# Stated orders of issue in the FFN and the recurrence of a hybrid HGRN2 and attention step

## The chip, the cores and the metric

The kernel runs on one core of a Trainium2 chip. The metric is device time in microseconds of one execution, the median of several; a separate profiled execution left the trace. The core's engines work side by side, each through its own instructions in a fixed order: TensorE (PE, with its weight loads PEld), VectorE (DVE), ScalarE (ACT), GpSimd (POOL) and SyncE (SP, which here issues transfers).

## What is computed

One layer of a diffusion backbone in float32 on 256 context ("prompt") and 1024 latent ("sample") tokens, width 1024: 1280 tokens in all. Cut to the parts that matter here:

```python
h = rms_norm(x, norm_mix_w) * (1 + sc1) + sh1          # sc, sh, g from adaln(c, w_ada)
z = h @ w_in                                            # hq, hf_fwd, hf_bwd, hi, hg, q, k, v, gl
o_a = block_attention(q, k_all, v_all)                  # latent: 512 cached + 1024 latent + context keys
# HGRN2, both directions, 4 heads of 128, chunks of 32:
f = lb + (1 - lb) * sigmoid(h_f);  k = 1 - f;  a = cumsum(log f) in the chunk
scores = tril((q e^a) (k e^-a)^T);   o = scores v + (q e^a) S;   S' = e^a_last S + (k e^(a_last - a))^T v
o_h = rms_norm(o_fwd + o_bwd) * silu(hg)
g = sigmoid(gl);  merged = g0 * (o_h @ w_ho) + g1 * (o_a @ w_ao)
x = x + g1 * (merged @ w_out)
x = x + g2 * (square(relu(norm2(x) @ w_ff1)) @ w_ff2)
y = rms_norm(x, final_norm_w)
```

Outputs are y for both kinds of token, the context's keys and values, and the final context states of the recurrence (`new_state_hgrn`, 2 directions x 4 heads).

## The kernel before

Every float32 operand of a large product is split into a high part (`hi`, on ACT) and a rest (`lo`, on DVE; both in `split`, L277 and L278), and each product is three matmuls: hi·hi, hi·lo, lo·hi (L306 to L308, L323 to L325). A weight block is loaded by `wraw` (1 MB, two buffers), split in halves by `w_oc` into `wsp` tiles (six buffers), and then used.

PE runs in the order in which the program is written. On DVE, ACT and POOL a scheduler sets the order when the kernel is built, from dependencies and priorities: `tc.high_priority(offset)` pulls the instructions inside it ahead. SP's order of transfers also comes from there, until the Strassen part, from where on it is written out. At run time each engine takes its instructions strictly in the order so set.

The stages, in us of the profiled execution's span:

- **Front**, 0 to 150: adaLN, first norm, projections for attention.
- **Attention**, 150 to 718: units of one head and 256 queries in 200 steps of 256 keys in all, each step with scores, maximum, exponential, transposition of the probabilities (`ps_t`, L735), their split (`pTh` on ACT, `pTl` on DVE L739) and the products with the values (L750, L751). At a unit's end the sum `oa` (L760) goes out. The work is a list of events in order of their step; between events `fill.to(...)` lets a *filler* put as many other matmuls on PE as its share of the total (277 estimated us) says. The filler `fz` here is the projections for the recurrence: `z_tok`, whose results pass through tiles `ze` (L849).
- **Recurrence**, 718 to 1003 (`hgrn`): 24 units `HUnit`, per head (direction, token tile) = (0,0), (0,1), (1,1), (1,0), (0,2), (1,2); tiles 0 and 1 are the latent tokens, 512 each, tile 2 the 256 context tokens. `prep` of unit i+1 is issued ahead of unit i's matmuls: it loads f (`uf`) and q (`uq`), runs two scans on DVE (`ucp`, the decay from the chunk's start, and `usf`, to its end), computes small tables of chunk products `um` and `udec`, k = 1 − f on POOL (L883), k·`usf` on POOL (L911), and that times two rows of `um`: one on POOL (in `uf`'s tile, for the scores), one on DVE (L907, in `usf`'s tile). The latter, called the *keyed product* in what follows, is transposed on PE by `keys_t` (L936) and copied by ACT to `ukt`. Two of three query products `uw` run on POOL, one on DVE. Then come the matmuls `scores` (masked to `usm`), `states_` (running states `ust`) and `out` (`uo`). The filler `fg` between them is the projection of the gates (`z_ch`).
- **Rest of the gates, merge, output projection**, 1003 to 1270.
- **FFN1, prompt pass**, 1270 to 1372: 16 turns i, each with two halves of 24 matmuls of a weight block just split; results squared and combined in `at` (DVE, L1378 to L1380). Beside it DVE and ACT form and split the sums of activations that the next stage needs: `sums1`, twelve parts, a part for every turn i = 3 to 14.
- **FFN1, Strassen part** for the latent tokens, 1372 to 1680: blocks of products over sums of blocks, X, Y and Z being banks of results; `u2` = Y + s1 (L1451) must be there before Y is used again (L1437).
- **FFN2**, 1680 to 2052, with chains P1 to P7 that end in residual additions, and the final norm (`square`, `final`) under and behind the last of them.

Of the kernel before, what the change touches and what calls it, by code (L numbers as in the profile page):

```python
# [15 lines left out]
P = 128  # L16
# [28 lines left out]
def build(ctx, tc, I, O, C):  # L45
# [230 lines left out]
    def split(hi, lo, raw):  # L276
        s_.activation(hi, raw, AF.Copy)  # L277
        v.tensor_tensor(lo, raw, f32(hi), op=ALU.subtract)  # L278
# [8 lines left out]

    def w_oc(raw, half, kcs=KC):

        hi, lo = wsp((P, kcs, P)), wsp((P, kcs, P))  # L290
        split(hi, lo, raw[:, :, half * P:(half + 1) * P])
        return hi, lo
# [37 lines left out]
    def z_ch(c0, consume):  # L330

        raw = wraw(I["w_in"], KC, c0)
        for half in range(2):
            wt = w_oc(raw, half)
# [323 lines left out]
    class Unit:  # L658
# [83 lines left out]
        def value(self, p2):  # L742
# [17 lines left out]
            v.tensor_tensor(oa, pv[d0:d0 + 64, 0:256], tm[d0:d0 + 64, 0:256], op=ALU.add)  # L760
# [4 lines left out]
    NORM = [g_, v]  # L765
    q_at, o_at = {}, {}
# [20 lines left out]
    def attention(fill):  # L787
# [68 lines left out]
    class HUnit:  # L856


        def __init__(self, h, d, t):
            self.h, self.d, self.t = h, d, t  # L860
            self.n, self.nb = TT[t][1], NB[t]

            self.zero = None if t < 2 else 0 if d == 0 else self.nb - 1

        def prep(self):
# [6 lines left out]
            c, e = S(name="ucp"), S(name="usf")  # L872
            if d == 0:
# [8 lines left out]
            k = self.k = f  # L882
            g_.tensor_scalar(k[:, 0:n], f[:, 0:n], -1.0, 1.0, op0=ALU.mult, op1=ALU.add)  # L883

# [7 lines left out]
            v.tensor_copy(out=Mf[:, 0:nb, 1:12:5], in_=Dv[:, :, 0:3])  # L892
            v.tensor_tensor(Mf[:, 0:nb, 2:8:5], Dv[:, :, 0:2], Dv[:, :, 1:3], op=ALU.mult)
            v.tensor_tensor(M[:, 0:nb, 0, 3], M[:, 0:nb, 0, 2], Dv[:, :, 2], op=ALU.mult)

            v.tensor_copy(out=M[:, 0:nb, 3, 2], in_=Dv[:, :, 3])
            for cc in (1, 0):
                v.tensor_tensor(M[:, 0:nb, 3, cc], M[:, 0:nb, 3, cc + 1], Dv[:, :, cc + 1], op=ALU.mult)
            v.reciprocal(M[:, 0:nb, 4, :], Dv)
            self.dec = T(4, "udec")  # L900
            v.tensor_tensor(self.dec[:, 0:nb], M[:, 0:nb, 3, 0], Dv[:, :, 0], op=ALU.mult)

            def mul4(out, in0, w, eng):
# [3 lines left out]
                eng.tensor_tensor(out[:, 0:n].rearrange("p (b c i) -> p b c i", c=4, i=32),  # L907
                                  in0[:, 0:n].rearrange("p (b c i) -> p b c i", c=4, i=32),
                                  mm.unsqueeze(3).broadcast_to([P, nb, 4, 32]), op=ALU.mult)

            g_.tensor_tensor(e[:, 0:n], k[:, 0:n], e[:, 0:n], op=ALU.mult)  # L911
            mul4(k, e, 4, g_)
            mul4(e, e, 3, v)
            self.ke = e
# [18 lines left out]
        def keys_t(self):  # L933
# [4 lines left out]
            with tc.high_priority(offset=400):  # L938
                s_.activation(self.kts[:, 0:self.nb], kt[:, 0:self.nb], AF.Copy)
# [73 lines left out]
    def hgrn(fill):  # L1013

        units = [HUnit(h, d, t) for h in range(4) for d, t in ((0, 0), (0, 1), (1, 1), (1, 0), (0, 2), (1, 2))]
# [8 lines left out]
        units[0].prep()  # L1024
        units[0].keys_t()
        for i in range(N + LATE):
            part = lambda x: fill.to((done + x * share[i]) / tot)
            if i + 1 < N:
                units[i + 1].prep()
            if i < N:  # L1030
# [6 lines left out]
                if u.t == 2:  # L1037
                    dma(O["new_state_hgrn"][u.d, u.h], st)
# [46 lines left out]
    fz = Filler(with_ada([*zh(0), *zh(1)], 0), 277.0)  # L1085
# [4 lines left out]
    fz.rest()  # L1090
# [3 lines left out]
    fg = Filler(with_ada([z_ch(GL + 256 * c, gl_consume(c)) for c in range(8)], 10), 194.0)  # L1094
    hgrn(fg)
# [263 lines left out]
    for i in range(NP):  # L1359
        r = raw1(i)  # L1360
        for half in range(2):
            j = 2 * i + half
            with tc.high_priority(offset=150 if i > 1 else 0):
# [18 lines left out]
        if 3 <= i < 15:  # L1382
            sums1((i - 3) // 3, (i - 3) % 3)
# [57 lines left out]
    for i in range(NP):  # L1441
# [9 lines left out]
        v.tensor_tensor(u2, Y, s1_, op=ALU.add)  # L1451
        if i == 0:
            for kb in range(4):
                fsplit("B22", kb, xa[1][kb + 4])
# [5 lines left out]
        if i == 0:  # L1460
            for kb in range(4):
                fsplit("T4", kb, xa[0][kb + 4])
# [212 lines left out]
    def final(b, put=store):  # L1675
# [4 lines left out]
        for i in range(2):  # L1680
            c = slice(i * 512, (i + 1) * 512)
            x = xt[b][:, c]
            v.scalar_tensor_tensor(x, x, rst[:, 0:1], fw[0][:, c], op0=ALU.mult, op1=ALU.mult)
            put(out_rows(b)[:, c], x)

# [102 lines left out]
```

## Time and profile before

| what | us |
|---|---|
| median of 3 runs | 2069.73 (2068.28 to 2074.16) |
| profiled execution | 2072.85 |
| its span in the trace | 2071.1 |
| PE busy in the span | 2018.6 (97%) |
| DVE, ACT, POOL busy | 1402.8, 921.9, 541.5 |
| matmuls | 12470 |

Busy time counts what an engine executes, not what it waits. The profiled execution was 3.1 us longer than the median run and its span 1.75 us shorter than its time.

### The profile page before, as it was taken

What the parts mean: (1) busy time and instruction counts of PE and PEld (TensorE: products, weight loads), DVE (VectorE), ACT (ScalarE), POOL (GpSimd) and SP (SyncE); (2) the same over time, 40 slices, a digit from 0 to 9 for tenths busy, and PEclk for the clock granted to TensorE, in tenths of its full rate; (3) what the DMA queues carried; (4) which work ended last, traced back from release to release, by engine and by line L of the source; (5) the groups of instructions that cost most, each with busy time, mean ns of one, the idle gap of its engine ahead of it and who ended that gap; (6) DMA issues with size and microseconds to landing.
All of it is one profiled execution on the core that took longest, in us unless ns stands there. A gap on an engine that the chain in (4) does not pass through costs nothing.

```text
span 2071.1 us, 33713 instructions
## 1 busy us (share of the span) xinstructions
PE 2018.6 (97%) x12470; PEld 1738.5 (84%) x12470; DVE 1402.8 (68%) x2660; ACT 921.9 (45%) x1877; POOL 541.5 (26%) x577
## 2 busy tenths in 40 slices
PE   6999999999999999999999999999999999999998
PEld 5798889988889988888888889988888888888886
DVE  4776676666676898778254636776666666577786
ACT  4635555555555522222221335554445444333442
POOL 1473233332332465445112100221221110000010
PEclk9999999999999999999999999999999999999999
DMA  9463222131221355454644533764444479555773
GB/s 305 146 190 102 71 76 73 55 120 54 67 77 56 102 184 163 156 159 153 202 143 147 178 112 105 233 198 161 147 155 147 154 275 364 155 155 180 229 254 125
DMA packets 220948, 317.38 MB, mean 153 GB/s; under 512 B 18504, under 2 KB 140192, under 8 KB 220784
## 3 DMA queue, kind: packets, MB, share of 16 engines
q1 hardware_dynamic: 208368, 275.58, 41.4%
q0 software_dynamic: 12416, 39.66, 5.4%
q8 instruction: 98, 1.61, 0.3%
q14 instruction: 66, 0.54, 0.1%
HBM read 229.43 MB, written 85.74 MB: 152 GB/s over the span
## 4 chain that ended last, share of the span: by engine, by line
PE 82%; DVE 7%; DMA 3%; ACT 2%; issue 2%; POOL 1%; SPq 0%; DVEq 0%; POOLq 0%; ACTq 0%
PE ps_g L306 7%; PE ps_g L308 7%; PE ps_g L307 7%; PE ps_s L694 4%; PE ps_t L735 3%; PE ps_g L1589 2%; PE ps_g L1591 2%; PE ps_g L1590 2%; DMA wraw<-in_w_in 2%; PE ps_s L1437 2%; PE ps_s L1439 2%; PE ps_s L1438 2%; PE ps_g L751 2%; PE ps_s L1589 2%; PE ps_s L1590 2%; PE ps_s L1591 2%
## 5 line engine op out<-in xcount | busy, mean ns | idle before, releaser
L306 PE MATMUL ps_g<-hs,wsp 128*128 128x512 f32 (+1 forms) x896 | 322.0, 359 | 0.4 <-DVE adas L186 0.4
L308 PE MATMUL ps_g<-hs,wsp 128*128 128x512 f32 (+1 forms) x896 | 309.7, 346 | 1.4 <-DVE wsp L278 1.4
L307 PE MATMUL ps_g<-hs,wsp 128*128 128x512 f32 (+1 forms) x896 | 309.3, 345 | 0.0
L713 POOL TENSOR_SCALAR pexp<-pexp,rs 128x512 f32<-128x512 f32 (+1 forms) x104 | 171.7, 1657 | 375.0 <-ACT pTh L738 190.8
L277 ACT ACTIVATE wsp<-wraw 128x1024 fp32r<-128x1024 f32 x110 | 109.6, 997 | 265.5 <-PE ps_g L307 80.3
L278 DVE TENSOR_TENSOR wsp<-wraw,wsp 128x1024 fp32r<-128x1024 f32 x110 | 134.6, 1225 | 122.4 <-ACT wsp L277 120.5
L308 PEld LDWEIGHTS ps_g<-hs,wsp 128*128 128x128 f32 x896 | 169.4, 189 | 23.2 <-DVE wsp L278 1.6
L306 PEld LDWEIGHTS ps_g<-hs,wsp 128*128 128x128 f32 x896 | 169.8, 189 | 21.5 <-issue 5.0
L307 PEld LDWEIGHTS ps_g<-hs,wsp 128*128 128x128 f32 x896 | 170.0, 190 | 15.1
L738 ACT ACTIVATE pTh<-ps_t 128x512 fp32r<-128x512 f32 x200 | 118.2, 601 | 127.4 <-PE ps_t L735 127.0
L695 DVE TENSOR_REDUCE mx<-ps_s 128x1 f32<-128x512 f32 (+1 forms) x208 | 136.9, 662 | 43.7 <-PE ps_s L694 42.9
L277 ACT ACTIVATE ah<-ar 128x640 fp32r<-128x640 f32 (+1 forms) x112 | 81.0, 723 | 190.3 <-PE ps_g L1590 102.3
L705 ACT ACTIVATE pexp<-ps_s,ngm 128x512 f32<-128x512 f32 (+1 forms) x208 | 137.2, 668 | 51.5 <-DVE ngm L699 47.1
L278 DVE TENSOR_TENSOR ah<-ar,ah 128x640 fp32r<-128x640 f32 (+1 forms) x112 | 89.8, 801 | 83.0 <-ACT ah L277 82.7
L739 DVE TENSOR_TENSOR pTl<-ps_t,pTh 128x512 fp32r<-128x512 f32 x200 | 134.8, 679 | 6.1 <-ACT pTh L738 5.9
L694 PE MATMUL ps_s<-Kl,Ql 128*128 128x512 f32 (+1 forms) x416 | 131.0, 413 | 0.8 <-ACT pexp L705 0.7
L735 PE MATMUL ps_t<-ident,pexp 128*128 128x128 f32 x800 | 120.5, 273 | 2.9 <-DVE pTl L739 2.6
L323 PE MATMUL ps_g<-wsp,hs 128*128 128x256 f32 x400 | 116.2, 291 | 0.0
L751 PE MATMUL ps_g<-pTl,Vl 128*128 128x256 f32 x400 | 105.7, 287 | 7.5 <-DVE pTl L739 7.4
L325 PE MATMUL ps_g<-wsp,hs 128*128 128x256 f32 x400 | 112.8, 282 | 0.0
L324 PE MATMUL ps_g<-wsp,hs 128*128 128x256 f32 x400 | 112.4, 281 | 0.0
L750 PE MATMUL ps_g<-pTh,Vl 128*128 128x256 f32 x400 | 105.5, 284 | 1.4 <-DVE um L892 0.7
(418 smaller groups left out, 5373.3 us busy)
## 6 DMA issues: line engine op xcount, KB each, us to landing
ar<-AF SPq DMA_DIRECT2D x112, 320.0 KB, 3.4
wraw<-in_w_ff SPq DMA_DIRECT2D x32, 1024.0 KB, 6.2
wr<-in_w_ff SPq DMA_DIRECT2D x128, 256.0 KB, 4.1
wraw<-in_w_in SPq DMA_DIRECT2D x18, 1024.0 KB, 6.2
wraw<-in_w_ada SPq DMA_DIRECT2D x16, 1024.0 KB, 5.5
AF<-a POOLq DMA_DIRECT2D x48, 256.0 KB, 2.8
AF<-t POOLq DMA_DIRECT2D x48, 256.0 KB, 2.3
wa<-in_w_ada SPq DMA_DIRECT2D x32, 256.0 KB, 5.9
```

The source lines that it names most:

```text
L277: s_.activation(hi, raw, AF.Copy)
L278: v.tensor_tensor(lo, raw, f32(hi), op=ALU.subtract)
L306: pe.matmul(out, hi[:, k, :], mh, start=(first and k == 0), stop=False)
L307: pe.matmul(out, hi[:, k, :], ml, start=False, stop=False)
L308: pe.matmul(out, lo[:, k, :], mh, start=False, stop=(last and k == kcs - 1))
L694: pe.matmul(pq[:, 0:n], self.qh[:, q0:q0 + P], K[self.g][var][self.kts[i]], start=(var == 0), stop=(var == 1))
L695: v.tensor_reduce(self.mx[j][:, i:i + 1], pq[:, 0:n], axis=AX.X, op=ALU.max)
L705: s_.activation(e[:, 0:n], self.ps.pop((j, i))[:, 0:n], AF.Exp, bias=self.mx[j], accum_out=self.sm[j][:, i:i + 1])
L713: NORM[(i + j) % len(NORM)].tensor_scalar(x, x, self.rs[j], None, op0=ALU.mult)
L735: pe.transpose(pt[:, a, j * P:(j + 1) * P], self.Ps[j][i][:, b * P:(b + 1) * P], ident)
L739: v.tensor_tensor(lo, pt, f32(hi), op=ALU.subtract)
L751: pe.matmul(pv[:, 0:256], V[self.g][kg][:, b, :], lo[:, a, :], start=False, stop=(k == last))
```

## The change

Six edits, none of which changes the set of matmuls:

1. *Attention.* The filler's total goes from 277 to 268 estimated us, and events in the last ten of 200 steps count double, so more of it comes late. What is left (`fz.rest`) is no longer put out at attention's end but between unit 0's `prep` and its `keys_t`. Unit 0's `prep` is ordered behind the last `oa` (`issue_after`: the instruction may not stand ahead of the named one, on the same engine). The first half of the first gate weight is loaded and split before the recurrence, at priority 600.
2. *Recurrence.* k = 1 − f goes to ACT. The keyed product is written into `uf`'s tile and the scores' operand (`self.k`) into `usf`'s, POOL's product last. What the keyed product needs stands first in `prep`, at priority 300 (from unit 2 on). `prep` of unit i+1 is ordered behind unit i's keyed product on DVE, and behind unit i's `ukt` copy on ACT.
3. *Stores of the new state* go by `store` (POOL's queue in this stage) and not by `dma` (SP's).
4. *FFN1, prompt pass.* The weight splits have priority 500 in place of 150, and each part of the sums is ordered behind the turn's last split.
5. *Strassen part.* `u2` has priority 100, and the DVE work of the splits B22 and T4 is ordered behind it (both in the same way).
6. *Last norm.* Half 1 of five token blocks is multiplied by the norm's weight on POOL (`weigh`) right after its squares are summed, and `final` scales such a half on ACT in place of DVE.

```diff
     def split(hi, lo, raw):
         s_.activation(hi, raw, AF.Copy)
-        v.tensor_tensor(lo, raw, f32(hi), op=ALU.subtract)
+        return v.tensor_tensor(lo, raw, f32(hi), op=ALU.subtract)
...
+    def z_ch(c0, consume, begun=None):
+        raw, wt = begun or (wraw(I["w_in"], KC, c0), None)
         for half in range(2):
-            wt = w_oc(raw, half)
+            if half or wt is None:
+                wt = w_oc(raw, half)
...
+        late = s0 - 8 - 2
+        def weight(a):
+            return a - e0 + max(0, a - late)
         for a, f, x in events:
-            fill.to((a - e0) / (e1 - e0))
+            fill.to(weight(a) / weight(e1))
...
+            first = tc.high_priority(offset=300 if self.i > 1 else 0)
+            first.__enter__()
 ...
-            k = self.k = f
-            g_.tensor_scalar(k[:, 0:n], f[:, 0:n], -1.0, 1.0, op0=ALU.mult, op1=ALU.add)
+            s_.activation(k[:, 0:n], f[:, 0:n], AF.Identity, scale=-1.0, bias=ones)
+            g_.tensor_tensor(e[:, 0:n], k[:, 0:n], e[:, 0:n], op=ALU.mult)
 ...
-            mul4(k, e, 4, g_)
-            mul4(e, e, 3, v)
-            self.ke = e
+            keyed[0] = mul4(k, e, 3, v)
+            self.ke = k
+            first.__exit__(None, None, None)
 ...
+            mul4(e, e, 4, g_)
+            self.k = e
...
-        units[0].prep()
+        with tc.issue_after(gone[0].ins):
+            units[0].prep()
+        before()
         units[0].keys_t()
...
-                units[i + 1].prep()
+                with ExitStack() as after:
+                    after.enter_context(tc.issue_after(copied[0].ins))
+                    after.enter_context(tc.issue_after(keyed[0].ins))
+                    units[i + 1].prep()
...
-                    dma(O["new_state_hgrn"][u.d, u.h], st)
+                    store(O["new_state_hgrn"][u.d, u.h], st)
...
-    fz = Filler(with_ada([*zh(0), *zh(1)], 0), 277.0)
+    fz = Filler(with_ada([*zh(0), *zh(1)], 0), 268.0)
...
-    fz.rest()
+    raw = wraw(I["w_in"], KC, GL)
+    with tc.high_priority(offset=600):
+        begun = [(raw, w_oc(raw, 0))] + 7 * [None]
+    hgrn(fg, fz.rest)
...
-            with tc.high_priority(offset=150 if i > 1 else 0):
+            with tc.high_priority(offset=500 if i > 1 else 0):
                 wt = w_oc(r, half)
...
-            sums1((i - 3) // 3, (i - 3) % 3)
+            with tc.issue_after(last_split[0].ins):
+                sums1((i - 3) // 3, (i - 3) % 3)
...
-        v.tensor_tensor(u2, Y, s1_, op=ALU.add)
+        with tc.high_priority(offset=100):
+            first = v.tensor_tensor(u2, Y, s1_, op=ALU.add)
...
+            with tc.issue_after(first.ins):
                 for kb in range(4):
                     fsplit("B22", kb, xa[1][kb + 4])
...
+            if i in ready.get(b, ()):
+                s_.activation(x, x, AF.Copy, scale=rst[:, 0:1])
+            else:
+                v.scalar_tensor_tensor(x, x, rst[:, 0:1], fw[0][:, c], op0=ALU.mult, op1=ALU.mult)
...
+    def weigh(b, i):
+        x = xt[b][:, i * 512:(i + 1) * 512]
+        g_.tensor_tensor(x, x, fw[0][:, i * 512:(i + 1) * 512], op=ALU.mult)
```

What this does to DVE's order, at three places. First the end of attention: the rows of DVE from the last but one unit's `oa` on, before (scans of unit 0 are L874 and L875):

```order
L739 TENSOR_TENSOR pTl_9097<-ps_t_9091,pTh_9096 128x512
L760 TENSOR_TENSOR oa_9067<-ps_g_9112,pvt_9117 64x256
L874 SCALAR_TENSOR_TENSOR ucp_9285<-R_9278,uf_9281 128x512
L875 SCALAR_TENSOR_TENSOR usf_9286<-uf_9281,R_9278 128x511
L876 MEMSET usf_9286 128x1
L849 SCALAR_TENSOR_TENSOR ze_9133<-ze_9133,ps_g_8939 128x512
L892 COPY um_9291<-ucp_9285 128x4x3
L739 TENSOR_TENSOR pTl_9144<-ps_t_9138,pTh_9143 128x512
L893 TENSOR_TENSOR um_9291<-ucp_9285 128x4x2
L896 COPY um_9291<-ucp_9285 128x4
```

and after, where the scans are L887 and L888, `oa` L763 and `pTl` L742:

```order
L742 TENSOR_TENSOR pTl_9096<-ps_t_9090,pTh_9095 128x512
L763 TENSOR_TENSOR oa_9116<-ps_g_9111,pvt_9117 64x256
L859 SCALAR_TENSOR_TENSOR ze_9135<-ze_9135,ps_g_9059 128x512
L763 TENSOR_TENSOR oa_9116<-ps_g_9147,pvt_9152 64x256
L887 SCALAR_TENSOR_TENSOR ucp_9169<-R_9156,uf_9165 128x512
L888 SCALAR_TENSOR_TENSOR usf_9170<-uf_9165,R_9156 128x511
L889 MEMSET usf_9170 128x1
L921 COPY um_9174<-ucp_9169 128x4x3
```

Unit 0's scans and tables stood among the last `pTl` and ahead of the last products; now they follow the last `oa`. On PE, 90 matmuls of `z_tok` and the last ada products now stand between attention's last value product and `keys_t` of unit 0.

Second, DVE in the recurrence where unit 14 begins; `usf_10966` and `um_10971` are unit 13's, `ucp_11120` and `um_11126` unit 14's. Before:

```order
L878 SCALAR_TENSOR_TENSOR ucp_11120<-R_9278,uf_11116 128x512
L879 SCALAR_TENSOR_TENSOR usf_11121<-uf_11116,R_9278 128x511
L880 MEMSET usf_11121 128x1
L899 RECIPROCAL um_11126<-ucp_11120 128x4x4
L892 COPY um_11126<-ucp_11120 128x4x3
L893 TENSOR_TENSOR um_11126<-ucp_11120 128x4x2
L896 COPY um_11126<-ucp_11120 128x4
L917 TENSOR_TENSOR uq_11117<-uq_11117,ucp_11120 128x512
L894 TENSOR_TENSOR um_11126<-um_11126,ucp_11120 128x4
L898 TENSOR_TENSOR um_11126<-um_11126,ucp_11120 128x4
L907 TENSOR_TENSOR usf_10966<-usf_10966,um_10971 128x512
```

After (unit 13's keyed product is written to `uf_10961`):

```order
L187 TENSOR_TENSOR modc_127<-adas_10915,cols_90 128x2x2
L907 TENSOR_TENSOR um_10970<-um_10970,ucp_10965 128x4
L913 TENSOR_TENSOR uw_10992<-uq_10962,um_10970 128x512
L926 TENSOR_TENSOR udec_10982<-um_10970,ucp_10965 128x4
L913 TENSOR_TENSOR uf_10961<-usf_10966,um_10970 128x512
L891 SCALAR_TENSOR_TENSOR ucp_11120<-R_9156,uf_11116 128x512
L965 TENSOR_TENSOR usm_11020<-ps_s_11003,mask0_113 128x512
L892 SCALAR_TENSOR_TENSOR usf_11121<-uf_11116,R_9156 128x511
```

The keyed product of unit 13 stood behind unit 14's scans and tables; now it stands ahead of them, here and at every unit.

Third, DVE in FFN1's prompt pass. Before (`t13`, `form` and `hs` belong to `sums1`, `wsp_15234` is the first split for turn 4):

```order
L1351 TENSOR_TENSOR t13_15693<-xa_14326,xa_14321 128x512
L1351 TENSOR_TENSOR t13_15927<-xa_14327,xa_14323 128x512
L1380 TENSOR_TENSOR at_15005<-ap_15006,at_15005 128x128
L278 TENSOR_TENSOR form_14869<-xa_14317,form_14866 128x512
L278 TENSOR_TENSOR hs_15615<-xa_14319,form_14867 128x512
L278 TENSOR_TENSOR wsp_15234<-wraw_15231,wsp_15233 128x1024
```

After, from the last split for turn 3 (`wsp_15188`) on:

```order
L278 TENSOR_TENSOR wsp_15188<-wraw_15152,wsp_15187 128x1024
L278 TENSOR_TENSOR hs_15224<-xa_14328,hs_15223 128x512
L1369 TENSOR_TENSOR t13_15227<-xa_14317,xa_14316 128x512
L278 TENSOR_TENSOR form_14862<-xa_14316,form_14858 128x512
L278 TENSOR_TENSOR wsp_15234<-wraw_15231,wsp_15233 128x1024
L1399 TENSOR_TENSOR at_15100<-ap_15101 128x256
L1400 TENSOR_TENSOR at_15100<-ap_15101,at_15100 128x128
L1401 TENSOR_TENSOR at_15100<-ap_15101,at_15100 128x128
L278 TENSOR_TENSOR wsp_15267<-wraw_15231,wsp_15266 128x1024
L1372 TENSOR_TENSOR t13_15227<-xa_14324,xa_14317 128x512
L278 TENSOR_TENSOR hs_15305<-t13_15227,hs_15304 128x512
L1373 TENSOR_TENSOR xa_14317<-xa_14324,t13_15227 128x512
```

Parts of the sums stood together, ahead of splits; now at most three of their instructions stand between two splits.

More of the change, by code (lines that the diff above doesn't have):

```diff
@@ L765, in build @@
     NORM = [g_, v]
+    gone, keyed, copied = [None], [None], [None]
     q_at, o_at = {}, {}
@@ L1461, in build @@
             for kb in range(4):
-                fsplit("T4", kb, xa[0][kb + 4])
+                with tc.issue_after(first.ins):
+                    fsplit("T4", kb, xa[0][kb + 4])
         prod(Z, w["S1"], "T1", True)
```

48 lines of the change are left out of this document (25 added, 23 removed).

## The prediction, made before the changed kernel ran

> **What bounds the kernel now.** I read the page first, then the span cut into its stages, then the waits of PE, then single places.
>
> Busy times of the page, and the busy times of each stage (columns: stretch in us, its length, then busy us and instructions of PE, PE's weight loads, DVE, ACT, POOL, the granted clock, DMA share, GB/s):
>
> ```profile
> PE 2018.6 (97%) x12470; PEld 1738.5 (84%) x12470; DVE 1402.8 (68%) x2660; ACT 921.9 (45%) x1877; POOL 541.5 (26%) x577
> ...
> 150.00:718.00 568.00, 558.38 (x4035) 505.55 (x4034) 393.26 (x862) 313.51 (x736) 181.88 (x112) 1.00 0.24 79
> 718.00:732.00 14.00, 10.13 (x96) 8.41 (x95) 13.83 (x29) 4.23 (x9) 8.07 (x8) 1.00 0.25 86
> 732.00:878.00 146.00, 145.59 (x1218) 122.71 (x1219) 123.25 (x275) 38.36 (x92) 80.82 (x91) 1.00 0.54 172
> 878.00:884.00 6.00, 3.78 (x20) 2.89 (x19) 6.00 (x14) 0.66 (x2) 5.67 (x6) 1.00 0.64 207
> 884.00:1003.00 119.00, 118.52 (x1017) 100.72 (x1016) 88.76 (x224) 31.62 (x84) 56.84 (x68) 1.00 0.50 156
> 1270.00:1372.00 102.00, 98.55 (x809) 97.42 (x808) 73.38 (x118) 68.48 (x124) 22.49 (x30) 1.00 0.71 220
> 1372.00:1386.00 14.00, 12.69 (x58) 10.28 (x57) 13.97 (x27) 7.40 (x14) 2.82 (x4) 1.00 0.30 97
> ...
> 2063.50:2071.10 7.60, 0.00 (x0) 0.00 (x0) 2.87 (x6) 0.72 (x2) 0.55 (x1) 0.68 0.36 136
> ```
>
> PE is the bound: 2018.6 of 2071.1 us at a clock of 1.00 in every stage shown that has matmuls. The change neither adds nor removes a matmul, so all that it can win is PE's idle time, 52.5 us in the span. Length minus PE's busy time says where that lies: attention 9.6, the passage to the recurrence (718 to 732) 3.9, six microseconds inside the recurrence 2.2 and all the rest of it 0.9, FFN1's prompt pass 3.4, the start of the Strassen part 1.3, the tail 7.6; the other 23 or so lie mostly before 150 and are not touched. In the passage and at 878 to 884 DVE is busy the whole time: PE waits for DVE's order, not for its total. The waits of PE name what was late (line waited for: us in total, times, longest), first for the whole span, then, below the dots, for 716 to 735 alone:
>
> ```profile
> PE ps_g L751 <- DVE pTl L739: 7.4, 10, 1.5
> PE ps_t L936 <- DVE usf L907: 3.2, 3, 2.2
> PE ps_t L735 <- DVE pTl L739: 2.6, 4, 0.9
> PE ps_s L308 <- DVE wsp L278: 2.0, 2, 1.5
> PE ps_g L308 <- DVE wsp L278: 1.4, 1, 1.4
> PE ps_s L1437 <- DVE u L1451: 1.3, 1, 1.3
> ...
> PE ps_g L751 <- DVE pTl L739: 1.7, 3, 1.1
> PE ps_t L936 <- DVE usf L907: 0.8, 1, 0.8
> PE ps_g L750 <- DVE um L892: 0.7, 1, 0.7
> PE ps_g L750 <- DVE oa L760: 0.7, 2, 0.4
> ```
>
> **Attention's end.** The last four rows are 3.9 us, the whole idle time of 718 to 732. DVE's timeline (start, us) shows why: unit 0's scans run in the middle of the last attention steps, and its keyed product `usf` (L907, what `keys_t` transposes) comes after unit 1's scans; the row above the dots is PE's pace just before.
>
> ```profile
> 704.00:718.00 14.00, 14.00 (x121) 14.00 (x120) 13.21 (x51) 10.48 (x31) 5.08 (x6) 1.00 0.30 105
> ...
> 716.57 1.23 DVE L874 TENSOR_TENSOR_SCAN ucp<-R,uf 128x512 f32<-128x512 f32 x1
> 717.71 1.20 DVE L875 TENSOR_TENSOR_SCAN usf<-uf,R 128x511 f32<-128x511 f32 x1
> 721.21 1.62 DVE L917 TENSOR_TENSOR uq<-uq,ucp 128x512 f32<-128x512 f32 x1
> 728.01 1.21 DVE L874 TENSOR_TENSOR_SCAN ucp<-R,uf 128x512 f32<-128x512 f32 x1
> 730.49 0.68 DVE L907 TENSOR_TENSOR usf<-usf,um 128x512 f32<-128x512 f32 x1
> ```
>
> In the new order unit 0 starts only after the last `oa`, and PE has 90 z matmuls and the ada ones between the last value and `keys_t`. At 14.00/121 = 0.116 us a matmul, the 90 alone are 10.4 us of cover. Under it must fit, after the last value: `oa` with its copy about 1.2 (estimated from the 0.4 of one DVE product), scans 2.4, k·e and the small products beside it with `uq` and `uw` 3 to 5, the keyed product 0.7 to 1.5: 7.3 to 10.1. So cover holds, by 0.3 to 3.1 us, and nothing of the 3.9 comes back here. Without that cover PE would wait for all 7 to 10. Term: −3.9, bounds −3.9 and −2.9 (chain 1 us over the upper end).
>
> The filler that covers this is taken out of the earlier steps: 190 of 200 steps get some 8% less filler (worked out from the two weights and the total that goes from 277 to 268), about 0.1 us a step, and the last ten twice as much. No row prices it. Attention has 14 waits for `pTl` over 200 steps; if each grows by 0.1, that is +1.4; if the redrawn pattern makes half as many again of their 10.0 us, +5; if the double filler removes waits as well, −3. DVE is 69% busy there and ACT 55%, so no engine becomes the bound, and I take +0.8, nearest to the growth of the waits that exist.
>
> The first half of the gate's weights is split ahead of the recurrence. Its load (1 MB) and split are the same work at another time; at 718 to 732 DMA is at 0.25, and it takes one of two raw buffers. Zero; without the earlier split, the filler's first matmul behind `keys_t` would wait for one split of about 1.2.
>
> **Recurrence.** Here are the durations (ns: minimum, median, maximum) of the products that change place, the queue of DVE behind POOL (us, times, longest), and DVE at 876 to 882:
>
> ```profile
> L883 POOL TENSOR_SCALAR uf<-uf x24: 398/618/1472, 719.2 to 983.2; 128x512 f32<-128x512 f32 x16, 128x256 f32<-128x256 f32 x8
> L911 POOL TENSOR_TENSOR usf<-uf,usf x24: 718/1279/2259, 721.0 to 985.7; 128x512 f32<-128x512 f32 x16, 128x256 f32<-128x256 f32 x8
> L907 POOL TENSOR_TENSOR uw<-uq,um x48: 612/1050/2027, 723.0 to 982.1; 128x512 f32<-128x512 f32 x32, 128x256 f32<-128x256 f32 x16
> L907 DVE TENSOR_TENSOR usf<-usf,um x24: 418/681/1537, 730.5 to 987.2; 128x512 f32<-128x512 f32 x16, 128x256 f32<-128x256 f32 x8
> L939 ACT ACTIVATE ukt<-ps_t x24: 376/598/602, 731.9 to 997.8; 128x512 f32<-128x512 f32 x16, 128x256 f32<-128x256 f32 x8
> L878 DVE TENSOR_TENSOR_SCAN ucp<-R,uf x12: 683/1214/1225, 742.2 to 979.8; 128x512 f32<-128x512 f32 x8, 128x256 f32<-128x256 f32 x4
> L898 DVE TENSOR_TENSOR um<-um,ucp x48: 150/162/1237, 724.0 to 981.6; 128x4 f32<-128x4 f32 x32, 128x2 f32<-128x2 f32 x16
> DVE usf L907 <- POOL uf L907: 15.1, 10, 2.3
> ...
> 876.90 1.20 DVE L879 TENSOR_TENSOR_SCAN usf<-uf,R 128x511 f32<-128x511 f32 x1
> 880.63 1.54 DVE L907 TENSOR_TENSOR usf<-usf,um 128x512 f32<-128x512 f32 x1
> ```
>
> At 876 unit 14's scans and small products stand ahead of unit 13's keyed product, which ends at 882.2; that is the wait of 2.2. The new edges keep every unit's scans behind the keyed product of the unit before, so it starts about 4 us sooner (scans 2.4, small products and `uq` 1.9): the 2.2 and the 0.2 that is left of L936 go, −2.4, between −2.4 and 0. The keyed product now writes another tile, so POOL's product with `um` comes after it: DVE's 15.1 us behind POOL, nearly all hidden today, leave the chain. k = 1−f goes from POOL (0.62) to ACT; its price there is bounded by the 0.38 to 0.60 of `ukt` copies of the same shapes, 0.6 on an engine that is a quarter busy. What it adds is a chain that cannot run ahead: `ukt` 0.6, k 0.6, two `uw` 2.1 ahead of k·e on POOL, k·e 1.3, keyed 0.7 to 1.5, so 5.3 to 6.1. PE's pace from unit to unit: 285 us for 16 long and 8 short units, the short ones at 0.6 of the long (shares 384 and 640), is 13.7 and 8.2. Slack is 2 us at the short ones. I put +0.5 for a unit or two that meets the upper rows. The stores of the new state go from SP's queue to POOL's: eight issues on an engine that is 55% busy, and nobody reads them; zero, at most the slack just named.
>
> Why small DVE products run at 0.15 and sometimes at 1.0 the rows show: their maximum is near POOL's median of 1.05. [...]
>
> **FFN1's prompt pass.** The 3.4 us idle are the two L308 rows, which fall between 1290 and 1330. DVE ran sums ahead of the split:
>
> ```profile
> 1296.93 1.28 DVE L1351 TENSOR_TENSOR t<-xa 128x512 f32<-128x512 f32 x2
> 1299.54 1.22 DVE L278 TENSOR_TENSOR wsp<-wraw,wsp 128x1024 fp32r<-128x1024 f32 x1
> ...
> wraw<-in_w_ff SPq DMA_DIRECT2D x32, 1024.0 KB, 6.2
> ```
>
> Now each part of the sums waits for the split before it, one part an i. A matmul takes 98.55/809 = 0.122 there, so an i of 48 gives DVE 5.85 us; it needs two splits 2.4, the three `at` about 1.0, and three sums 1.9, so 5.3. The load's round goes load 6.2, then hi (about 1.0 on ACT) and lo twice, 10.6 us for two i, against PE's 11.7. It fits with 10%, hence −3.4 +0.5, bounds −3.4 and +0.6 (a wait of 0.3 in each of 14 i's).
>
> **Strassen start.** The wait of 1.3 is `u` behind ten splits; `u` now goes first and these follow. Four splits at 0.6 (B22) come first, for matmuls some 7 us later, and then 3.8 for T4, read later still (estimates from the products of that size), so −1.3, bounds −1.3 and 0.
>
> **Last norm.**
>
> ```profile
> 2066.60 1.41 DVE L1683 SCALAR_TENSOR_TENSOR x<-x,frst,fwb 128x512 f32<-128x512 f32 x2 [0.73 <-POOL frst L166]
> 2067.38 0.99 SPq L101 DMA_DIRECT2D out_y_prompt<-x  x2
> ```
>
> One of two DVE products becomes an ACT scaling beside the other. That frees 0.7, of which the two stores, issued one after the other in 0.99, leave 0 to 0.5: −0.3. The multiplication by the weight goes to POOL under matmuls, five times about 1.3.
>
> **Sum:** −3.9 +0.8 −2.4 +0.5 −2.9 −1.3 −0.3 = −9.5. The profiled execution took 2072.85 (span 2071.1 and 1.75 around it), so 2063.3; it lies 3.1 above the median of 2069.73, so 2060.2 for a median.
>
> **Rivals.**
> - *Attention's waits are redrawn for the worse.* For it: the 10.0 us of `pTl` waits show a chain without much slack; against: no engine above 69%. Five microseconds in place of 0.8: 2064.4, inside the bound of no change.
> - *FFN1 only moves its waits.* The load's round is 10% short of PE's; if loads take 7 us, as with DMA at 0.71 they may, the waits stay and the term is about 0: 2063.1 alone, 2064 or more with any other miss.
> - *The order does not take the waits away*: another row on DVE or POOL (`ze`, `ust`, which wait for PE) stands ahead of the keyed products, and the −3.9 and the −2.4 fall out: 2066.5. Against it: at attention's end all such rows read what PE makes before the cover or in it.
> - *Slower: the chain through ACT and POOL in the recurrence.* At the maxima of the rows (k·e 2.26, `uw` 2.03 twice, keyed 1.54, `ukt` and k 1.2) it is 9.1 us, 0.9 over the pace of the 8 short units: +7. If DVE also takes three small products at 1.0 instead of 0.15 in each unit, 12 units add 30 us to the 123 of 146: +7 more, and the 2.4 are not won. That gives 2076.6, and decides from about 2 us of extra wait a unit. Against it: medians, not maxima, held in 24 units before, and POOL has one operation less. [...]
>
> **How the numbers follow.** What this kernel's measurement can tell from no change is about 0.3%, 6.2 us, so faster means below 2063.5. The forecast case has 0.62 (alone 2055 to 2063.5), attention 0.13, FFN1 0.09, no effect 0.08, slower chain 0.08. Half of FFN1's case still counts as faster: 0.66, same 0.26, slower 0.08. Low 2053.5 is the sum with attention at −3 and its 0.5s gone, and 2 us for the run; high 2068.5 holds the cases up to "no effect".
>
> **What would show it.** Right: no row of L950 (before L936) above 0.3 us in the waits, L310 without `wsp`, none at `u`, and PE idle of attention at 10 to 11. Wrong: attention's idle time above 13, new rows of L950 behind POOL's k·e, or DVE rows waiting for POOL L904 with PE's rows behind them.

## The result and the profile after

The changed kernel took 2054.91 us (median of 6 runs, 2053.5 to 2055.6); the kernel before took 2072.98 beside it (6 runs, 2068.28 to 2075.08). The ratio is 0.9914, with a 95% interval of [0.9903, 0.9925]. The forecast was 2060.2 with a range of 2053.5 to 2068.5. Direction and range held, near the range's lower end. The forecast gain was 9.5 us; that of the medians is 18.1, nearly twice as much. Three executions with a granted clock of 0.56 to 0.75, one of `x_ffn` and two of the kernel before, are left out of all comparisons below.

Stages of the changed kernel (columns as in the prediction; with an earlier end, the passage is 712 to 727, the recurrence 727 to 990, FFN1's prompt pass 1258 to 1358):

```profile
150.00:712.00 562.00, 553.71 (x3999) 500.44 (x3998) 393.59 (x867) 313.95 (x739) 181.10 (x112) 1.00 0.24 78
712.00:722.00 10.00, 10.00 (x91) 9.87 (x93) 9.94 (x16) 2.46 (x4) 6.22 (x6) 1.00 0.47 147
722.00:727.00 5.00, 5.00 (x80) 3.96 (x72) 5.00 (x12) 2.12 (x4) 2.91 (x3) 1.00 0.44 157
727.00:740.00 13.00, 11.95 (x95) 9.61 (x87) 10.33 (x21) 2.05 (x4) 7.80 (x8) 1.00 0.77 245
740.00:868.00 128.00, 128.00 (x1080) 108.98 (x1077) 106.88 (x252) 40.31 (x98) 69.39 (x74) 1.00 0.53 165
868.00:990.00 122.00, 121.86 (x1032) 103.44 (x1030) 94.28 (x232) 38.45 (x98) 60.19 (x67) 1.00 0.50 159
1258.00:1358.00 100.00, 100.00 (x821) 99.24 (x820) 78.31 (x123) 71.23 (x127) 23.34 (x31) 1.00 0.77 233
1358.00:1372.00 14.00, 14.00 (x64) 11.58 (x63) 12.98 (x24) 5.99 (x11) 2.08 (x3) 1.00 0.37 111
2045.50:2053.10 7.60, 0.00 (x0) 0.00 (x0) 2.23 (x5) 1.44 (x3) 0.55 (x1) 0.76 0.18 69
```

PE is busy through the passage, FFN1 and the start of the Strassen part; in the recurrence 1.05 us are left at 737, a wait for `adas` (before, 0.4 us at 830). PE's waits from 150 to 716, that is, all of attention, where PE is idle for 8.3 us:

```profile
PE ps_g L754 <- DVE pTl L742: 4.0, 10, 0.8
PE ps_t L738 <- DVE pTl L742: 1.8, 3, 0.9
PE ps_t L738 <- DVE pexp L716: 1.3, 3, 0.7
```

The same matmul can be found in both traces by its number in PE's order (the order differs only between matmul 900 and 5050). The difference of its start shows where time went. Here each column is a stretch between two such matmuls, in us against the kernel before; the last column counts stretches of halved clock between 30 us and the last matmul, which the next section explains.

```
kernel     front attention+passage recurrence FFN1 Strassen rest | last matmul  halved
before       0.0        0.0           0.0      0.0    0.0    0.0 |     0.0        2
changed     -1.8       -7.1          -2.6     -4.4   -1.6   -0.7 |   -18.2        0
x_attn      -0.7       -2.6          -0.1     +1.1   +1.3   -0.9 |    -1.9        2
x_rec       -1.7       -3.2          -4.5      0.0   +2.9   +0.2 |    -6.3        2
x_ffn       -2.6       -2.3          +2.1     -4.4   -1.6   -0.4 |    -9.2        1
x_recffn    +0.3       -3.1          -4.5     -4.4   -1.6   +0.1 |   -13.3        3
x_unif      +1.2       -6.1          -3.2     -4.4   -1.6   -0.2 |   -14.3        3
x_noedge    -0.8       -2.1          -4.5     -4.4   -1.6   -0.4 |   -13.7        2
x_nopace    -0.7       +4.3          -4.3     -4.4   -1.6   +0.4 |    -6.4        5
```

The front has the same order in all of them, so its column, -2.6 to +1.2, is what chance does to one execution. The time after the Strassen part ("rest") has the same order too where edit 6 is the same.

**A stretch of halved clock.** One-microsecond slices of the kernel before, in attention:

```profile
489.00:490.00 1.00, 1.00 (x5) 0.56 (x3) 1.00 (x2) 0.93 (x2) 0.00 (x0) 1.00 0.00 0
490.00:491.00 1.00, 0.12 (x1) 0.00 (x0) 0.97 (x3) 0.00 (x0) 0.00 (x0) 1.00 0.00 0
491.00:492.00 1.00, 0.63 (x4) 0.42 (x4) 0.94 (x3) 0.41 (x1) 0.00 (x0) 1.00 0.00 0
492.00:493.00 1.00, 0.58 (x2) 0.30 (x2) 0.27 (x1) 1.00 (x5) 0.00 (x0) 0.86 0.00 0
493.00:494.00 1.00, 1.00 (x3) 0.82 (x3) 0.56 (x1) 1.00 (x4) 0.00 (x0) 0.50 0.00 0
...
495.00:496.00 1.00, 1.00 (x5) 0.80 (x4) 0.85 (x5) 0.00 (x0) 0.71 (x1) 0.50 0.00 0
496.00:497.00 1.00, 1.00 (x7) 0.84 (x6) 0.47 (x3) 0.00 (x0) 1.00 (x2) 0.93 0.00 0
```

After 1.7 us of idle time within 3 us, the granted clock is 0.50 for 3.4 us. PE shows as busy there (matmuls of 512 columns, L306 to L308, start 0.43 us apart from 494.10 on, against 0.23 from 487.42 on), so 1.7 us more are lost that no idle time shows. The kernel before had two such stretches (59.0 to 62.4 and 492.5 to 495.9), the changed one none: 3.4 of the 18 us between these two executions. The first of the two lies in the front, which the change leaves alone, so its half of the 3.4 is chance. What sets off such a stretch is taken up in *What a wait costs beyond its length* below.

### The profile page after: what moved, and what is told of

Read it like the earlier page. It is cut to its first block, busy times and chain, and to the rows that moved or that the text cites. A ratio compares the mean times of both kernels' runs of the same rounds, so it can differ in the third digit from the quotient of the medians.

```text
span 2053.1 us, 33691 instructions
## 1 busy us (share of the span) xinstructions
PE 2012.3 (98%) x12470; PEld 1736.1 (85%) x12470; DVE 1405.3 (68%) x2655; ACT 938.5 (46%) x1906; POOL 546.1 (27%) x566
## 4 chain that ended last, share of the span: by engine, by line
PE 62%; DVE 2%; issue 1%; ACT 0%; DMA 0%; POOL 0%; POOLq 0%; ACTq 0%; DVEq 0%
PE ps_g L308 5%; PE ps_g L309 5%; PE ps_g L310 5%; PE ps_g L1614 2%; PE ps_g L1616 2%; PE ps_g L1615 2%; PE ps_s L1460 2%; PE ps_s L1461 2%; PE ps_s L1459 2%; PE ps_s L1614 2%; PE ps_s L1615 2%; PE ps_s L1616 2%; PE ps_t L1614 2%; PE ps_t L1615 2%; PE ps_t L1616 2%; PE ps_s L308 2%
## 5 line engine op out<-in xcount | busy, mean ns | idle before, releaser
L308 PE MATMUL ps_g<-hs,wsp 128*128 128x512 f32 (+1 forms) x896 | 322.2, 360 | 1.1 <-DVE adas L186 1.0
L278 DVE TENSOR_TENSOR wsp<-wraw,wsp 128x1024 fp32r<-128x1024 f32 x110 | 139.9, 1272 | 114.8 <-ACT wsp L277 114.4
L308 PEld LDWEIGHTS ps_g<-hs,wsp 128*128 128x128 f32 x896 | 169.6, 189 | 22.3 <-issue 4.6
L742 DVE TENSOR_TENSOR pTl<-ps_t,pTh 128x512 fp32r<-128x512 f32 x200 | 135.9, 681 | 14.1 <-ACT pTh L741 13.9
L754 PE MATMUL ps_g<-pTl,Vl 128*128 128x256 f32 x400 | 105.9, 287 | 4.0 <-DVE pTl L742 4.0
L738 PEld LDWEIGHTS ps_t<-ident,pexp 128*128 128x128 f32 x800 | 93.6, 140 | 14.1 <-issue 4.0
```

The costliest lines, as they stand in the source:

```text
L278: return v.tensor_tensor(lo, raw, f32(hi), op=ALU.subtract)
L308: pe.matmul(out, hi[:, k, :], mh, start=(first and k == 0), stop=False)
L738: pe.transpose(pt[:, a, j * P:(j + 1) * P], self.Ps[j][i][:, b * P:(b + 1) * P], ident)
L742: v.tensor_tensor(lo, pt, f32(hi), op=ALU.subtract)
```

## Experiments

All ratios below are to the kernel before, run beside them. Edits are given against the kernel named.

**One part alone.** `x_attn` keeps only the attention edit (1), `x_rec` only 2 and 3, `x_ffn` only 4, 5 and 6; the rest is as before.

> The kernel before with the attention edit alone (later filler, cover, order edge, early split). Theory P (as forecast): about -3.1 us, all of it at the passage, attention itself no better. Theory Q (the later filler also removes waits inside attention): -6 to -8 us, of which 4 at the passage and 1 to 2 of idle time between 150 and 700; and where the profile shows no stretch of halved clock there, up to 1.7 of that is chance.

> The kernel before with the recurrence edits alone (order of prep, k on ACT, stores on POOL). As forecast: about -2 us, the wait of 2.2 us at unit 13 gone. If the gain there is bound up with the passage, or a wait at another unit comes in its place: 0 or slower.

> The kernel before with the edits from FFN1 on alone (splits ahead of sums, u2 first, last norm). As forecast by idle time: -2.9 -1.3 -0.3 = -4.5 us. If a stall costs more than the idle time that the trace shows (pipe and weight loads to refill): -6 us, with the pace of the halves 2.9 us everywhere.

Measured: `x_attn` 2071.38, ratio 1.0001 [0.9992, 1.0009]; `x_rec` 2067.34, 0.9980 [0.9971, 0.9988]; `x_ffn` 2064.29, 0.9960 [0.9947, 0.9973]. The attention edit alone gives nothing, against both theories. By the table its trace gains 2.6 us up to the passage's end and loses 2.4 in FFN1 and at the Strassen start, whose order it does not touch (`u` is late by 2.6 us in place of 1.3). PE's waits from 700 to 900, and DVE:

```profile
PE ps_t L946 <- DVE usf L917: 5.5, 2, 3.3
```

```profile
712.79 1.71 DVE L884 TENSOR_TENSOR_SCAN ucp<-R,uf 128x512 f32<-128x512 f32 x1
...
720.59 1.43 DVE L884 TENSOR_TENSOR_SCAN ucp<-R,uf 128x512 f32<-128x512 f32 x1
...
726.23 0.67 DVE L917 TENSOR_TENSOR usf<-usf,um 128x512 f32<-128x512 f32 x1
```

Without the recurrence's edits, unit 0's keyed product still stands behind unit 1's scans. It ends 14 us after unit 0's first scan, later than the cover of 11 us. PE waits 3.3 us, and a stretch of halved clock follows (727.8 to 731.3). `x_ffn` gains in its own stages what the changed kernel gains, 4.4 and 1.6 us, as its second case said. `x_rec` gains 4.5 in the recurrence, twice its forecast; the changed kernel keeps 2.6 of that. Of the 1.9 between them 1.2 are the wait for `adas`: 1.0 to 1.1 us in the kernels that have cover, order edge and recurrence edits together, none in those that have the recurrence edits without cover or without edge. `x_ffn` has one halved stretch behind the wait of 2.2 at 877, `x_rec` one behind `u` at 1378 (2.6 us of wait, 1.3 more than before), and these are most of the +2.1 and the +2.9 of the table.

**All but the attention edit**

```diff
-    fz = Filler(with_ada([*zh(0), *zh(1)], 0), 268.0)
+    fz = Filler(with_ada([*zh(0), *zh(1)], 0), 277.0)
...
-            fill.to(weight(a) / weight(e1))
+            fill.to((a - e0) / (e1 - e0))
...
-        with tc.issue_after(gone[0].ins):
-            units[0].prep()
+        units[0].prep()
...
+    fz.rest()
...
-    with tc.high_priority(offset=600):
-        begun = [(raw, w_oc(raw, 0))] + 7 * [None]
+    if True:
+        begun = 8 * [None]
...
-    hgrn(fg, fz.rest)
+    hgrn(fg, lambda: None)
```

> The changed kernel with the attention edit taken back (277 spread evenly, no cover, no order edge, no early split); everything else stays. The attention edit alone gave nothing. Theory I (the cover is worth something only where the keyed product comes first): this kernel is 4 to 6 us slower than the changed one, so about -11 against the kernel before, and waits for pTl, um and oa come back at the passage. Rival (the attention edit gives nothing in company either, and the 17 us are made by the rest): within 1.5 us of the changed kernel.

Measured: 2060.19, ratio 0.9947 [0.9934, 0.9961]. Against the changed kernel that is 5.3 us slower, and waits for `pTl`, `um` and `oa` are back at the passage (3.0 us together), so theory I holds: the edit that gives nothing alone gives something in company. How much is less sure than the 5.3. The two aligned traces differ by 4.9 us: 4.0 in attention and passage (1.7 of it a halved stretch) less 1.9 in the recurrence are the edit's own, and 2.9 lie in the front and the rest, where both kernels have the same order. So 2 to 5 us.

**The attention edit taken apart.** `x_nopace` leaves the order edge and takes the cover (277, evenly spread); `x_noedge` leaves the cover and takes the edge; `x_unif` leaves both and spreads the 268 evenly.

> The changed kernel with the filler's total at 277 and evenly spread, as before, but with unit 0 still ordered behind the last oa: the edge without the cover. As forecast (7 to 10 us between the last value and the first keyed product): PE waits 7 to 9 us at the first keys_t, and the time is 7 to 9 us above the changed kernel, less what the filler gives back in the steps (1 to 3), and one stretch of halved clock more (1.7). If the edge costs little without cover: within 3 us of the changed kernel.

> The changed kernel without the order edge that holds unit 0's prep behind the last oa; the later filler, its cover of 90 z matmuls and the early split stay: the cover without the edge. If the cover alone takes the passage's wait away (keys_t comes 11 us after the last value whatever DVE did before): keys_t does not wait, but oa, pTl and um rows wait again as in the kernel before, 1.5 to 3 us in all, and the time is 1.5 to 3 us above the changed kernel. If the cover also hides those, since PE has filler for them: within 1 us.

> The changed kernel with the filler's 268 spread evenly (no double weight in the last ten steps), so the main steps get about 4% more filler than in the changed kernel. If only the total sets the cover: the same time as the changed kernel within 1 us. If the late weight itself removes waits in the last steps: 1 to 3 us more. If the thinner filler in the main steps costs anything: 1 us less.

Measured: `x_nopace` 2067.26 (0.9979 [0.9969, 0.9989]), `x_noedge` 2060.03 (0.9951 [0.9939, 0.9964]), `x_unif` 2058.96 (0.9932 [0.9920, 0.9943]). Waits of PE, first `x_nopace`, then `x_noedge`:

```profile
PE ps_t L950 <- DVE uf L913: 9.3, 1, 9.3
```

```profile
PE ps_g L753 <- DVE oa L763: 3.3, 2, 2.3
```

Without the cover the whole chain shows: 9.3 us, and three halved stretches (728 to 739). The first of them falls into the wait itself, so they cost 3.0 us more: 12.3 us, which is what the medians show (2067.26 to 2054.91) and more than was expected with one stretch. Without the edge unit 0's scans stand in the last steps again, `oa` is late twice, by 3.3 us in all, and one halved stretch follows (707 to 711): 5.0 us in attention and passage, 5.1 by the medians. So the edge without cover costs 7 us against `x_recffn`, the cover without edge gives nothing, and both together, with the keyed product first, give the gain.

`x_unif` is 4.1 us above the changed kernel by the medians (the intervals of the ratios overlap), 3.9 by the traces, 3.0 of which lie in the front. Its attention and passage are 1.0 us longer, with a halved stretch (1.7) in them, behind the longest of these waits (150 to 716):

```profile
PE ps_g L754 <- DVE pTl L742: 5.5, 8, 1.5
```

The kernels with the even filler (`before`, `x_rec`, `x_ffn`, `x_recffn`, `x_nopace`, `x_unif`) all have one or two waits for `pTl` of 1.3 to 1.5 us in attention, and two of the six a halved stretch there. In the eight with the late weight none is above 0.9, and none has such a stretch before the last steps. So the late weight takes the longest waits away; what that saves in time beyond the stretches is not measured.

**What lengthens the scans**

```diff
-            mul4(e, e, 4, g_)
+            mul4(e, e, 4, v)
```

> The changed kernel with the last product of each unit (scores' operand) on DVE in place of POOL. If POOL's product holds up the scan that runs beside it: the second scan's median falls from 2.0 and 1.47 us back to 1.2. If the scans are long for another reason (ACT's k, the loads): 1.5 to 2.0 as in the changed kernel. Time: DVE gets 24 products of 0.42 to 0.68 more and loses 24 times up to 0.8 of scan time, PE is not waiting, so within 1 us of the changed kernel by either.

Measured: 2056.21, ratio 0.9927 [0.9908, 0.9947]. The second scan (backward units) in ns, before, changed, `x_lock`:

```profile
L879 DVE TENSOR_TENSOR_SCAN usf<-uf,R x12: 675/1194/1222, 743.4 to 982.1; 128x511 f32<-128x511 f32 x8, 128x255 f32<-128x255 f32 x4
```

```profile
L892 DVE TENSOR_TENSOR_SCAN usf<-uf,R x12: 675/2003/2011, 734.3 to 969.4; 128x511 f32<-128x511 f32 x8, 128x255 f32<-128x255 f32 x4
```

```profile
L892 DVE TENSOR_TENSOR_SCAN usf<-uf,R x12: 680/1194/1197, 736.2 to 969.5; 128x511 f32<-128x511 f32 x8, 128x255 f32<-128x255 f32 x4
```

It is POOL's product, released by the same keyed product as the scans, that makes the second ones 0.8 us longer. One unit of the changed kernel:

```profile
733.17 1.22 DVE L891 TENSOR_TENSOR_SCAN ucp<-R,uf 128x512 f32<-128x512 f32 x1
734.30 2.01 DVE L892 TENSOR_TENSOR_SCAN usf<-uf,R 128x511 f32<-128x511 f32 x1
...
733.33 1.90 POOL L913 TENSOR_TENSOR usf<-usf,um 128x512 f32<-128x512 f32 x1 [0.81 <-DVE uf L913]
```

The first scan starts just ahead of the product and keeps its 1.22 us; the second starts while the product runs and ends 1.1 after it. Of the eight long second scans of the changed kernel's backward units seven took 2.00 to 2.01 us and one 1.42. The prediction's row of the scans before had a narrow spread (L878: 1214 ns in the median, 1225 at most); in the old order they did not start together with that product, which came ahead of the keyed one. The longer scans cost no time that shows: with them at 1.19 `x_lock` is no faster.

**What a wait costs beyond its length.** In the changed kernel, ACT repeats a copy of one tile in seven blocks of the Strassen part (`m` 13 to 17 times in `x_stall`, 10 to 12 in `x_stall2`), so that `u2` and with it PE are late (`m` stands for the table of the blocks and their numbers):

```diff
         s_.activation(s1_, X, AF.Copy)
+        for _ in range(m.get(i, 0)):
+            s_.activation(s1_, s1_, AF.Copy)
```

> The changed kernel with 13 to 17 extra copies of one tile on ACT in each of seven blocks of the Strassen part, so that PE is held up there by some 1 to 4 us each time. Theory C (a stretch of about 1.7 us of PE's idle time within some 4 us halves the clock for 3.4 us, by chance of where it falls): some of the stalls of 1.7 us and more are followed by such a stretch, each worth 1.7 us, none of those below 1.2. Rival (the two stretches of the kernel before came from something else, such as power or time since the start): none is followed by one.

> As x_stall, with 10 to 12 copies, so that by its steps of 0.65 us a copy PE is held up by about 1.5, 2.2, 2.8, 2.2, 1.5, 2.2 and 2.2 us. Theory C with chance: of the seven, one to four are followed by a stretch of halved clock of 3.4 us, the longer ones more readily; the time is the changed kernel's plus 14.6 us of waits and 1.7 for each stretch. Rival (a fixed threshold near 1.7): the five of 2.2 and more all are, the two of 1.5 are not.

Measured: 2107.03 and 2072.03 (single runs). Waits of PE, in that order:

```profile
PE ps_s L1459 <- DVE u L1476: 33.7, 7, 6.1
```

```profile
PE ps_s L1459 <- DVE u L1476: 14.7, 7, 2.8
```

In `x_stall` the waits came out at 3.5 to 6.1 us, longer than aimed at, and all seven are followed by one or two halved stretches. In `x_stall2` they are 0.4 twice and 2.8 five times, 14.7 us in all, and one of the five is followed by a stretch. That is within theory C's one to four; the rival, a fixed threshold near 1.7 us of wait, falls. The bill closes: the span is 17.0 us above the changed kernel's, of which the waits are 14.7 and the stretch 1.7.

What decides between five stalls alike to 0.05 us is where they fall. The trace notes every change of the granted clock, and in each of the 14 traces all of them lie, to 3 ns, on a grid of 3.41 us, which starts at another time in every execution. Two of the five stalls, cut at that grid; the first (1443.12 to 1445.90) is divided between two windows, the second (1525.49 to 1528.27) lies mostly in one, and the window behind it is halved:

```profile
1441.04:1444.45 3.41, 2.08 (x10) 1.38 (x8) 0.96 (x2) 3.11 (x6) 0.00 (x0) 1.00 0.41 101
1444.45:1447.87 3.42, 1.97 (x9) 1.63 (x10) 1.40 (x2) 1.54 (x4) 0.54 (x1) 1.00 0.77 265
...
1522.97:1526.38 3.41, 2.52 (x12) 1.75 (x10) 0.69 (x1) 3.11 (x6) 0.00 (x0) 1.00 0.27 62
1526.38:1529.79 3.41, 1.52 (x7) 1.25 (x8) 1.83 (x2) 1.99 (x4) 0.54 (x1) 1.00 0.74 254
1529.79:1533.21 3.42, 3.42 (x10) 2.68 (x9) 0.67 (x1) 0.00 (x0) 0.00 (x0) 0.50 0.18 69
```

The other three stalls leave at most 1.68 us of idle time in a window, the last one here 1.89. Over all traces, from 150 us to the last matmul, there are 7779 windows at full clock. The 13 with 1.9 us of idle time or more were all followed by a halved one, of the 13 with 1.5 to 1.9 three were, and of the rest none. So in these traces about half a window of idle time (1.9 of 3.41 us) halved the next, and most of the chance lay in where a wait met the grid.

**What is left in attention.** Some of the waits for `pTl` in the changed kernel's attention stand right behind a weight split of 1.21 us on DVE: three of thirteen, with 1.7 of the 5.8 us. `x_half` does the splits of `w_kh` in two halves each; `x_pool` does their second parts on POOL. These are 8 of the 19 splits in attention; the others come from `w_oc` and stay as they are.

```diff
-        split(hi, lo, raw[:, half * 4:half * 4 + 4, :])
+        for k in (0, 2):
+            split(hi[:, k:k + 2], lo[:, k:k + 2], raw[:, half * 4 + k:half * 4 + k + 2, :])
```

```diff
-        split(hi, lo, raw[:, half * 4:half * 4 + 4, :])
+        x = raw[:, half * 4:half * 4 + 4, :]
+        s_.activation(hi, x, AF.Copy)
+        g_.tensor_tensor(lo, x, f32(hi), op=ALU.subtract)
```

> The changed kernel with the weight splits of attention's filler done in two halves each (512 columns in place of 1024), aimed at what is left: half of the waits for pTl in attention stand behind a split of 1.21 us on DVE. If a split's length is what makes them: the 5.8 us of pTl waits fall to about 3, and the time by 2 to 3 us. If the halves run back to back, or the 0.14 us that each costs more moves other work: within 1 us, or slower.

> The changed kernel with the second parts of the same splits on POOL in place of DVE. If DVE's queue is what makes the pTl waits: they fall to about 3 us, and the time by 2 to 3. Rival: POOL is slower at it (2.1 to 2.6 us by its products of 512 columns) and its normalisation of the probabilities comes late; waits for pexp L716 grow, and the time is the same or up to 5 us longer.

Measured: `x_half` 2054.83 (0.9912 [0.9897, 0.9926]), `x_pool` 2053.07 (0.9906 [0.9890, 0.9923]). Waits of PE from 150 to 716, `x_half` and then `x_pool`:

```profile
PE ps_g L755 <- DVE pTl L743: 2.4, 8, 0.6
PE ps_t L739 <- DVE pTl L743: 1.8, 3, 0.9
PE ps_t L739 <- DVE pexp L717: 1.8, 4, 0.7
```

```profile
PE ps_g L756 <- DVE pTl L744: 2.6, 8, 0.6
PE ps_t L740 <- DVE pTl L744: 1.5, 2, 0.9
PE ps_t L740 <- DVE pexp L718: 0.6, 2, 0.4
```

The waits for `pTl` fall from 5.8 to 4.2 and 4.1, less than to 3. Of the three waits behind a split the one of 0.80 us is gone; the two others (0.3 and 0.6) stand in both kernels as before, behind splits that the edit leaves alone. So whether a split's length makes them is only in part tested. `x_half` is as fast as the changed kernel. With POOL the waits for `pexp` fall too, from 1.3 to 0.6, against the rival. `x_pool` has the lowest median of all kernels run, but its interval overlaps the changed kernel's, so it is not shown to be faster; in the traces its attention and passage are 4.2 us shorter, but that trace is of its fastest execution (2050.78).

## Why the prediction was right, and where its sizes were off

Forecast and measured, by term; the measured ones are from the aligned traces, the halved stretches apart.

| term | forecast | measured |
|---|---|---|
| attention and passage | -3.9 +0.8 | -5.4 |
| recurrence | -2.4 +0.5 | -2.6 |
| FFN1's prompt pass | -3.4 +0.5 | -4.4 |
| Strassen start | -1.3 | -1.6 |
| last norm and the rest | -0.3 | -0.6 |
| halved clock | none | -3.4 |
| sum | -9.5 | -18.0 |

- *Passage.* The mechanism held. The keyed product is ready at 720.13 and `keys_t` (L950) starts at 722.78, so the cover held by 2.65 us:

```profile
710.77 0.28 PE L754 MATMUL ps_g<-pTl,Vl 128*128 128x256 f32 x1
...
711.50 0.43 DVE L763 TENSOR_TENSOR oa<-ps_g,pvt 64x256 f32<-64x256 f32 x1 [0.29 <-ACT pvt L762]
711.95 1.70 DVE L887 TENSOR_TENSOR_SCAN ucp<-R,uf 128x512 f32<-128x512 f32 x1
...
719.45 0.68 DVE L913 TENSOR_TENSOR uf<-usf,um 128x512 f32<-128x512 f32 x1
...
722.78 0.66 PE L950 MATMUL ps_t<-ident,uf 128*128 128x128 f32 x4
```

From the last value product (L754, which ends at 711.05) to the keyed product's end it is 9.1 us, inside the 7.3 to 10.1 of the prediction, and without cover PE waited 9.3. The step that the text lacked is that the cover needs the recurrence's edit: it took unit 0's keyed product to be ready by the new order and did not say that by the old one it comes 14 us after the scan.
- *Attention's +0.8* had the wrong sign. `pTl` waits were to grow by a tenth each; from 150 to 716 they fell from 8.3 us to 5.8, and the longest from 1.5 to 0.9. In the other kernels with attention's old order they come to 6.8 to 7.6 us, and in `x_unif` to 6.3 with the longest at 1.5, so some of the fall is chance and the longest waits go with the late weight; why it removes them is not shown. The sign set for this, attention idle for 10 to 11 us, was missed on the good side: 8.3.
- *FFN1, Strassen and recurrence* were mis-sized mainly because the terms were read off idle time. A row of PE (0.28 us in the first two below) ends later than the next matmul starts. Before FFN1's first wait stands:

```profile
1298.88 0.28 PE L306 MATMUL ps_s<-hs,wsp 128*128 128x256 f32 x1
1298.99 0.28 PE L307 MATMUL ps_s<-hs,wsp 128*128 128x256 f32 x1
1300.81 0.38 PE L308 MATMUL ps_s<-hs,wsp 128*128 128x256 f32 x1 [1.53 <-DVE wsp L278]
```

Starts are 0.12 apart and then 1.82: 1.70 are lost where the idle time says 1.53. Over the three waits that make the 3.4 us this gives 3.9; the other 0.5 of the 4.4 is spread over waits too short to be listed. The +0.5 kept there for new waits was not needed: FFN1 is busy for 100.00 of 100 us. In the recurrence the edits gain 4.5 where the idle time said 2.4 (`x_rec`), and a wait did appear (`adas`, 1.05, which costs 1.2), at another place than the one that the +0.5 was kept for; the 2.6 is the balance of the two.
- *Last norm.* Two scalings now run beside each other, but the end did not move: from `frst` to the end of the span it is 5.08 us before (2066.02 to 2071.1) and 5.06 after (2048.04 to 2053.1). The -0.3 for the tail was wrong; what the table shows there (-0.7 ahead of the last matmul) is within what that stretch does from trace to trace, -0.9 to +0.4 in the table.
- *The missing term* was the clock. The text saw a clock of 1.00 in each stage shown and did not cut the stages finely enough to see 0.50 for 3.4 us. Of the 8.5 us between forecast and the two traces it is 3.4, attention 2.3, the short reading of idle time and the reserves kept beside it 2.5, and the rest 0.3. The 3.4 is that of one pair of executions. The mean granted clock of 56 executions of the kernel before, beside the experiments, is 0.9968, that of the changed kernel's six 0.9975: 6.7 and 5.1 us of clock lost (the end behind the last matmul included), so about 1.5 us in the usual execution. The median of the 56 is 2071.2, which makes the usual gain some 16 us, and the other terms of the table add up to 14.6.
- *The rivals.* The slower chain through POOL did not come: DVE waits for POOL's k·e (16.6 us in 11 times), PE never for what follows from it.
- The priority of 500 for FFN1's splits changes no row of any engine's order: built with 150 in its place, the changed kernel is the same program. Edit 4 is the order edge of the sums alone.

## What to carry to other kernels

Measure a wait of the bounding engine from start to start, not by its idle time, and add what it can set off: here a wait of PE of 1.5 us and more could cost 1.7 us of halved clock on top, depending on where it fell. Taking away waits also made the time steadier (2053.5 to 2055.6 against 2068.3 to 2075.1, six executions each). Edits that fill one gap are to be tried together as well as apart: the attention edit was worth 0 alone and 2 to 5 us in company. One trace of each kernel shows which waits are gone, but where a stretch of the same order differs by 2 us between two traces, a difference of 2 us elsewhere needs more than one execution. A queue's order that is decided when the kernel is built is worth reading row by row before a priority is turned.

## What the runs showed of the hardware

- In each of the 14 traces the granted clock changed only on a grid of 3.41 us, which started at another time in every execution. Of the 7779 windows of the grid at full clock, those in which PE was idle for 1.9 us or more were always followed by one at 0.50 (13 of 13), those with less than 1.5 never, those between them in 3 of 13 cases. A halved window cost up to 1.7 us, worked out from 3.41 us at 0.50, and showed as busy time. So one stall of 2.8 us halved the clock (1526.38 in `x_stall2`) and another, alike but divided between two windows (1443.12 to 1445.90), did not.
- The second scan of the changed kernel's backward units (`usf` from `uf` and `R` on DVE, L892) took 2.00 us in the median, where it started while a product on POOL ran that was released with the scan before it. With that product on DVE (`x_lock`) it took 1.19, and 1.19 in the order of the kernel before (L879): the duration of one order did not hold in the other.
